# A down projection whose VectorE and ScalarE work is pinned to the program's order, with six weight-row buffers

## The chip, the cores and the metric

The kernel runs on one core of a Trainium2 chip. The metric is the device time of one execution in microseconds (us). Before the change it is 1452.64 us, the median of three runs (1451.81 to 1452.75).

## What is computed

One decoder layer for 256 tokens of width 2048, all in float32. A norm and an input projection feed a state-space branch and an attention branch; an output projection joins them to `x`; a convolutional feed-forward follows, and a last norm. The change touches only the end:

```
h = rms_norm(x, ffn_norm_w)
u = causal_depthwise_conv(h @ w_up, ffn_conv_w, ffn_conv_b)   # 2048 -> 2 x 5632
gate, val = split(u)
x = x + (silu(gate) * val) @ w_down                           # 5632 -> 2048
return rms_norm(x, final_norm_w)
```

## The kernel before, in words

**Precision.** A float32 product is made of three TensorE products. ScalarE rounds a 128 x 1024 block of weights into a high part (`whi`, line 1193), VectorE subtracts that from the block for the low part (`wlo`, line 1199), and TensorE adds (activation high) x (weight high), (activation low) x (weight high) and (activation high) x (weight low). The pair "high part, then low part" of one block is its *preparation*.

**Steps.** The whole program is one list of steps. A step loads a weight block, prepares it, and multiplies by it. The main loop at the end of the program walks the list. At step i it issues the loads up to step i + 7, the preparation of step i + 3 (`AHEAD`), then the step's own `pre` hook, its matmuls, its `post` hook, and then some pieces of side work taken from a queue of generators (`tick`, two pieces for most steps):

```
for i in range(n):
    loads_to(i + LOADS)
    while pi < n and pi <= i + AHEAD and i > 2:
        for f_ in steps[pi].prep: f_()
        pi += 1
    ... s.pre(); s.mm(); s.post(); tick(...)
```

There are four row buffers for the loaded blocks (`RAWS`) and four pairs of high and low buffers (`SPLITS`). So the preparation of step i + 3 writes the buffers that the matmuls of step i - 1 read.

**Who sets the order.** The program's order is only a wish. A scheduler in the language orders each engine's instructions ahead of the run by its own estimate of when each is ready. Each engine then works through its fixed list. An instruction made through a `Pinned` handle (lines 70 to 91) can be tied behind the instruction traced before it on its engine: TensorE's handle `T` always does this, `V` (VectorE), `A` (ScalarE) and `S` (SyncE's DMA queue) do it while the list `pin` isn't empty. Before the change `pin` holds something for the first seven steps only. The loads of the down projection's rows (lines 1178 and 1244), the final norm's weight (line 1152) and the output's stores (line 1396) are issued through `nc.sync`, not through `S`.

**The down projection.** `w_down` has 44 blocks of 128 rows; each block is taken in two halves of 1024 columns, so there are two passes over the rows, here called the first and the second half. Two neighbouring blocks make a pair, and there are 22 pairs in each half. A pair marked p in `orders` is two plain steps of 12 matmuls of 512 columns each (`prod_steps`). A pair marked s (6 in the first half, 7 in the second) is worked by a scheme with seven products in place of eight (`seven_steps`), in four steps a, b, c, d of 6, 6, 6 and 3 matmuls. Their preparations are chained: `t1` (line 1248) subtracts within the first row ahead of a's high part, `t23` (lines 1253 and 1254) makes the block `q` ahead of c's, and `t4` (line 1259) makes `r` ahead of d's; b has no such step. In the second half the order of pairs is pp, s p, four times s pp, s p, s ppp.

**Side work there.** `gather` and `sums` (lines 1281 to 1288, then a split at lines 95 and 96) make sums of activations for the seven s pairs, in three pieces each, 21 in all. A p step of the first half takes one piece while its row number is under 36, else two; s steps take none. `merge` (lines 1337 and 1338) adds the s pairs' banks into `x1` in four pieces after the last s pair of each half. `down_evac` (line 1360) adds a bank into `x1` and `square` (line 1354) sums its squares; `post0` does both four times at the end of the first half. `weigh` (line 1368) multiplies two quarters of `x1` by the final norm's weight `fnw`, which line 1427 scales by -0.5 first. `last_mm` ends the second half in an order of its own, with `finish_tokens` (lines 1385 to 1396) writing the output.

**Places.** `hcatf0` to `hcatf3`, the up projection's input, lie in four 8 KB places (per partition) H0 to H3. In the down projection H1 holds the scratch `tq`, H2 and H3 hold sums, and H0 holds `fnw`. Each pair's activations `act0` to `act21` have a 4 KB place of their own.

Of the kernel before, what the change touches and what calls it, by code (L numbers as in the profile page):

```python
# [10 lines left out]
F32 = mybir.dt.float32  # L11
F32R = mybir.dt.float32r
# [4 lines left out]
P = 128  # L17
D = 2048
L = 256
# [6 lines left out]
NHID = 256  # L26
NSH = 32
EPS = 1e-6
AHEAD, LOADS, WARM, FILL = 3, 7, 7, 2
RAWS, SPLITS, LATE = 4, 4, 4  # L30
R_SSM = 1.75
RATE = {"b": 2, "c": 2, "dt": 2, "x": 2, "ck": 1, "cv": 1, "q": 1.55, "z": 1.55}
# [11 lines left out]
def hymba_kernel(  # L44
# [22 lines left out]
    def wide(slot, shape, dtype, name):  # L67
        return gp.tile(shape, dtype, tag=f"H{slot}", name=name)
# [103 lines left out]
    small = lambda tag: gp.tile([P, 4, 3], F32, tag=tag, name=tag)  # L172
    for tag in ("nm1", "sm0", "sm1"):
        small(tag)
    hc = [wide(i, [P, 4, 2, L], F32R, f"hcat{i}") for i in range(4)]
    gp.tile([P, 16], F32, tag="pad", name="gpad")
    hcat = lambda k: hc[k // 4][:, k % 4]

    mixc = const.tile([P, NK], F32, name="mixc")

# [853 lines left out]
    x1 = [None] * 4  # L1034
    xsq = const.tile([P, NT, 4], F32, name="xsqs")
    hc2 = [None] * 4
    hcat2 = lambda k: hc2[k // 4][:, k % 4]

    def transpose_x1(c):
        yield from pause(WAIT["x1"])  # L1040
        for kk in range(4):
            k = 4 * c + kk
            if kk == 0:
                hc2[c] = wide(c, [P, 4, 2, L], F32R, f"hcatf{c}")
            ps = aux_bank()
            for t in range(NT):
                T.transpose(ps[:, t * P:(t + 1) * P], x1[c][:, t, kk * P:(kk + 1) * P], ident)
            split_scaled(hcat2(k)[:, 0], hcat2(k)[:, 1], ps[:, 0:256], pcol(O_FN + k))
            yield
# [97 lines left out]
    fnw = []  # L1147
    tqs = []

    def load_fnw():  # L1150
        ft = wide(0, [P, 4, 512], F32, "fnw")
        nc.sync.dma_start(ft.rearrange("p c e -> p (c e)"), final_norm_w.partition_broadcast(P))
        fnw.append(ft)

    def prod_steps(src, np_, pr, act, banks, first, last):

        for kl in range(2):
            k = 2 * pr + kl

            def mm(hf, w, k=k, kl=kl, ids=((0, 0), (0, 1), (1, 0), (1, 1))):  # L1160
                hv, lv = w
                x_ = banks["x"]
                if not x_:
                    x_.extend(banks["xb"]() for _ in range(4))
                for t, n in ids:
                    for hl in range(2):
                        T.matmul(x_[2 * t + n], act(k)[:, hl, t * P:(t + 1) * P], hv[:, n],
                                 start=(first and kl == 0 and hl == 0), stop=False)
                for t, n in ids:
                    T.matmul(x_[2 * t + n], act(k)[:, 0, t * P:(t + 1) * P], lv[:, n],  # L1170
                             start=False, stop=(last and kl == 1))

            s = Step()

            def load(k=k, s=s):
                raw = stage.tile([P, 1024], F32, tag="raw", name="raw", bufs=RAWS)
                s.raw = raw.rearrange("p (n c) -> p n c", n=2)
                nc.sync.dma_start(raw, src[k * P:(k + 1) * P, np_ * 1024:(np_ + 1) * 1024])

            s.load = load  # L1180
            s.prep = halves(s, lambda s=s: s.raw)
            s.mm = lambda s=s, mm=mm: mm(0, s.w)
            s.mm_ids = lambda ids, s=s, mm=mm: mm(0, s.w, ids=ids)
            s.k = k
            s.post = s.pre = None
            s.ticks = 2 - (np_ == 0 and k < 36)
            steps.append(s)
# [16 lines left out]
    def seven_steps(src, np_, pr, parts, banks, first, last):  # L1204

        st = {}  # L1210

        def product(bank, a_, w, n, x_first=False):
            (hv, lv), (ah, al) = w, a_()
            kw = dict(start=False, stop=False)
            T.matmul(bank, ah, hv[:, n], start=x_first, stop=False)
            T.matmul(bank, al, hv[:, n], **kw)
            T.matmul(bank, ah, lv[:, n], start=False, stop=last and any(bank is b for b in banks["y"]))

        def y(i):
            if not banks["y"]:  # L1220
                banks["y"].extend(banks["yb"]() for _ in range(4))
            return banks["y"][i]

        def mm_a(s):
            product(y(0), lambda: parts["a11"], s.w, 0, first)
            product(y(1), lambda: parts["s1"], s.w, 1, first)

        def mm_b(s):
            product(banks["x"][0], lambda: parts["a12"], s.w, 0)
            product(banks["x"][1], lambda: parts["s4"], s.w, 1)  # L1230

        def mm_c(s):
            product(y(2), lambda: parts["s2"], s.w, 0, first)
            product(y(3), lambda: parts["s3"], s.w, 1, first)

        def mm_d(s):
            product(banks["x"][2], lambda: parts["a22"], s.w, 0)

        def load_row(kl):
            def load():  # L1240
                raw = stage.tile([P, 1024], F32, tag="raw", name="raw", bufs=RAWS)
                st[kl] = raw.rearrange("p (n c) -> p n c", n=2)
                k = 2 * pr + kl
                nc.sync.dma_start(raw, src[k * P:(k + 1) * P, np_ * 1024:(np_ + 1) * 1024])
            return load

        def t1():
            V.tensor_tensor(st[0][:, 1], st[0][:, 1], st[0][:, 0], op=ALU.subtract)  # L1248

        def t23():  # L1250
            q_ = tqs[0][:, 0]
            st["q"] = q_
            V.tensor_tensor(q_[:, 0], st[1][:, 1], st[0][:, 1], op=ALU.subtract)
            V.tensor_tensor(q_[:, 1], q_[:, 0], st[0][:, 0], op=ALU.subtract)

        def t4():
            q_ = tqs[0][:, 1]
            st["r"] = q_
            V.tensor_tensor(q_[:, 0], st[1][:, 0], st["q"][:, 0], op=ALU.subtract)  # L1259

        def ready():
            while "a22" not in parts:
                tick(1)

        for mm, load, pre, key, n in ((mm_a, load_row(0), t1, 0, 2), (mm_b, load_row(1), None, 1, 2),
                                      (mm_c, None, t23, "q", 2), (mm_d, None, t4, "r", 1)):
            s = Step()
            s.load = load
            hl = halves(s, lambda key=key: st[key], n)
            s.prep = ((pre,) if pre else ()) + hl  # L1270
            s.mm = lambda s=s, mm=mm: mm(s)
            s.post = None
            s.pre = ready if key == 0 else None
            s.ticks = 0
            steps.append(s)
# [88 lines left out]
    def weigh():  # L1364
        for c in range(2):
            for t in range(NT):
                yield
                V.tensor_tensor(x1[c][:, t], x1[c][:, t], fnw[0][:, c], op=ALU.mult)
        yield

    fpart = const.tile([P, NT], F32, name="fpart")
# [6 lines left out]
    def finish_tokens(t, ssq_, more):  # L1378

        v, p_, f = (const.tile([P, 1], F32, name=f"fin{n_}{t}") for n_ in "vpf")
        r_ = const.tile([P, 1], F32, name=f"finr{t}")
        A.activation(r_, ssq_, AF.Sqrt, bias=more, scale=1.0 / D)
        V.tensor_scalar(v, ssq_, 1.0 / D, more, op0=ALU.mult, op1=ALU.add)
        V.reciprocal(r_, r_)
        V.scalar_tensor_tensor(p_, r_, v, r_, op0=ALU.mult, op1=ALU.mult)
        V.scalar_tensor_tensor(f, p_, -3.0, r_, op0=ALU.add, op1=ALU.mult)
        for q, (c, c0, n) in enumerate(((2, 0, 256), (0, 0, 512), (2, 256, 256), (1, 0, 512), (3, 0, 512))):  # L1390
            o_ = x1[c][:, t, c0:c0 + n]
            if c < 2:
                A.activation(o_, o_, AF.Copy, scale=f)
            else:
                V.scalar_tensor_tensor(o_, o_, f, fnw[0][:, c, c0:c0 + n], op0=ALU.mult, op1=ALU.mult)  # L1395
            nc.sync.dma_start(out[t * P:(t + 1) * P, c * 512 + c0:c * 512 + c0 + n], o_)

    orders = ["ppp" + "spp" * 5 + "sppp", "pp" + "sp" + "spp" * 4 + "sp" + "sppp"]
# [23 lines left out]
            banks["n"] = len(steps)  # L1422

    steps[n_down].pre = start_down
    steps[down[0]["n"]].pre = lambda: aux.append(weigh())
    steps[n_down + 2].pre = load_fnw
    steps[n_down + 36].pre = lambda: [A.activation(fnw[0][:, c], fnw[0][:, c], AF.Copy, scale=-0.5) for c in range(4)]
    steps[n_down + 64].pre = lambda: load_sqrt(fsq[:, 0, 0:1])
    last = steps[-LATE:]
    for i, s_ in enumerate(last[:-1]):  # L1430
# [69 lines left out]
    steps[6].post, steps[3].post = steps[3].post, None  # L1500
    credit = 0.0
    for i in range(n):
        loads_to(i + LOADS)
        while pi < n and pi <= i + AHEAD and i > 2:
            if steps[pi].late and pi > i + AHEAD - 1:
                break
# [3 lines left out]
        s = steps[i]  # L1510
        if s.pre:
            s.pre()
        if i < 3:
            s.mm_pass(0)
            steps[pi].prep[0]()
            split_x(range(4 * i + 4, 4 * i + 8))
            steps[pi].prep[1]()
            pi += 1
            s.mm_pass(1)
            if i == 1:  # L1520
                square_x((1,))
        else:
            s.mm()
# [45 lines left out]
```

## Time and profile before

| | |
|---|---|
| median of the runs | 1452.64 us |
| the profiled execution | 1451.33 us, its span 1449.7 us |
| TensorE (PE) busy | 1437.4 us, 99% |
| weight load into TensorE (PEld) | 1346.8 us, 93% |
| VectorE (DVE) busy | 1101.1 us, 76% |
| ScalarE (ACT) busy | 844.7 us, 58% |
| GpSimd (POOL) busy | 3.6 us |
| mean granted TensorE clock | 0.998 |

The span runs from the first to the last instruction; the execution takes 1.6 us more. The down projection's matmuls begin at 1207.05 us of the span, its second half at 1323.6 us, and the last matmul starts at 1440.64 us. Matmuls overlap one another, so that a busy TensorE isn't TensorE at its fastest: what shows a stall is the distance between the starts of matmuls.

### The profile page before, as it was taken

To read this page: it belongs to the slowest core of one execution; us is meant where nothing else is said; L and a number is where in the kernel's file an instruction comes from. 1 tells how busy PE (TensorE), PEld (TensorE's weight loads), DVE (VectorE), ACT (ScalarE), POOL (GpSimd) and SP (SyncE) were. 2 spreads that over 40 slices of the span, in tenths; PEclk is the share of its full clock that TensorE was granted. 3 is DMA by queue.
4 is the path that set the end of the run, shared out by engine and by line. 5 is a ranking of instruction groups with operands and counts; after the bars stand their busy time and mean duration, and the time that the engine had idled before them with its cause. 6 is when DMAs were issued, how large, how long until landed. Compare 5 with 4: busy or idle time off the path is not lost.

```text
span 1449.7 us, 26506 instructions
## 1 busy us (share of the span) xinstructions
PE 1437.4 (99%) x10512; PEld 1346.8 (93%) x10512; DVE 1101.1 (76%) x1733; ACT 844.7 (58%) x1281; POOL 3.6 (0%) x19
## 2 busy tenths in 40 slices
PE   9999999999999999999999999999999999999997
PEld 9999998989999998888899999999999998788886
DVE  7899699757797898555477777777777779878877
ACT  6677456556687696444355555555555556555554
POOL 1000000000000000000000000000000000000000
PEclk9999999999999999999999999999999999999999
DMA  8657667775544547566566666666666665665654
GB/s 274 186 181 241 182 212 234 237 216 159 156 137 140 161 134 231 188 189 192 178 195 194 198 192 193 197 192 193 197 193 192 198 192 191 205 204 186 213 193 145
DMA packets 222699, 278.76 MB, mean 192 GB/s; under 512 B 13176, under 2 KB 186864, under 8 KB 222448
## 3 DMA queue, kind: packets, MB, share of 16 engines
q1 hardware_dynamic: 220800, 272.59, 61.4%
q10 hardware_dynamic: 1776, 4.50, 0.9%
q8 instruction: 82, 1.34, 0.4%
q14 instruction: 41, 0.34, 0.1%
HBM read 274.92 MB, written 2.13 MB: 191 GB/s over the span
## 4 chain that ended last, share of the span: by engine, by line
PE 93%; DVE 3%; ACT 2%; DMA 1%; issue 1%; DVEq 0%; ACTq 0%; SPq 0%
PE mm L89 79%; PE aux L89 13%; DMA raw<-in_w_down_dram 1%; DVE wlo L1199 1%; ACT p L813 1%; ACT whi L1193 0%; DVE wlo L348 0%; DVE p L789 0%; DVE x L1395 0%; ACT L813 0%; ACT junk L1354 0%; DVE x L1337 0%; DVE pt L96 0%; ACT whi L342 0%; DVE tq L1259 0%
## 5 line engine op out<-in xcount | busy, mean ns | idle before, releaser
L342 ACT ACTIVATE whi<-raw 128x1024 fp32r<-128x1024 f32 x408 | 430.8, 1058 | 415.7 <-PE mm L89 360.9
L348 DVE TENSOR_TENSOR wlo<-raw,whi 128x1024 fp32r<-128x1024 f32 x408 | 496.4, 1220 | 222.8 <-ACT whi L342 214.1
L89 PE MATMUL mm<-hcatf,whi 128*128 128x256 f32 x2816 | 348.5, 277 | 0.0
L89 PEld LDWEIGHTS mm<-hcatf,whi 128*128 128x128 f32 x2816 | 332.6, 188 | 0.1
L89 PE MATMUL mm<-hcat,whi 128*128 128x256 f32 (+1 forms) x2336 | 294.8, 279 | 0.0
L89 PEld LDWEIGHTS mm<-hcat,whi 128*128 128x128 f32 (+1 forms) x2336 | 280.9, 188 | 2.7 <-issue 0.7
L89 PE MATMUL mm<-hcatf,wlo 128*128 128x256 f32 x1408 | 188.5, 277 | 0.0
L89 PEld LDWEIGHTS mm<-hcatf,wlo 128*128 128x128 f32 x1408 | 172.8, 188 | 0.0
L89 PE MATMUL mm<-hcat,wlo 128*128 128x256 f32 (+1 forms) x1168 | 159.8, 278 | 0.0
L89 PEld LDWEIGHTS mm<-hcat,wlo 128*128 128x128 f32 (+1 forms) x1168 | 144.5, 187 | 0.2 <-DVE wlo L89 0.2
L1193 ACT ACTIVATE whi<-raw 128x1024 fp32r<-128x1024 f32 x88 | 91.8, 1057 | 66.9 <-DVE raw L1248 19.0
L1199 DVE TENSOR_TENSOR wlo<-raw,whi 128x1024 fp32r<-128x1024 f32 x88 | 105.7, 1221 | 13.0 <-ACT whi L1193 11.9
L89 PE MATMUL aux<-whi,act 128*128 128x512 f32 (+1 forms) x306 | 78.0, 388 | 1.2 <-ACT whi L1193 1.2
L89 PE MATMUL mm<-whi,act 128*128 128x512 f32 (+1 forms) x286 | 74.2, 387 | 0.0
L89 PEld LDWEIGHTS aux<-whi,act 128*128 128x128 f32 x306 | 57.1, 188 | 13.2 <-ACT whi L1193 1.5
L390 DVE TENSOR_TENSOR u<-mm,bc 128x256 f32<-128x256 f32 x88 | 37.3, 424 | 36.9 <-PE mm L89 35.6
L89 PE MATMUL mm<-whi,ya 128*128 128x512 f32 x256 | 64.3, 394 | 0.0
L89 PEld LDWEIGHTS mm<-whi,act 128*128 128x128 f32 x286 | 53.5, 188 | 11.0
L89 PE MATMUL mm<-whi,ys 128*128 128x512 f32 x256 | 63.2, 390 | 0.0
L89 PEld LDWEIGHTS mm<-whi,ys 128*128 128x128 f32 x256 | 48.1, 188 | 9.9
L89 PEld LDWEIGHTS mm<-whi,ya 128*128 128x128 f32 x256 | 47.5, 188 | 9.6
L89 PE MATMUL aux<-wlo,act 128*128 128x512 f32 (+1 forms) x153 | 43.8, 388 | 0.0
(324 smaller groups left out, 1516.1 us busy)
## 6 DMA issues: line engine op xcount, KB each, us to landing
raw<-in_w_up_dram SPq DMA_DIRECT2D x176, 512.0 KB, 4.5
raw<-in_w_in_dram SPq DMA_DIRECT2D x160, 512.0 KB, 3.8
raw<-in_w_down_dram SPq DMA_DIRECT2D x88, 512.0 KB, 4.9
raw<-in_w_out_dram SPq DMA_DIRECT2D x64, 512.0 KB, 4.7
acq<-acum_d ACTq DMA_DIRECT2D x8, 512.0 KB, 5.5
raw<-in_cmp_w_k_dram SPq DMA_DIRECT2D x8, 512.0 KB, 5.1
raw<-in_cmp_w_v_dram SPq DMA_DIRECT2D x8, 512.0 KB, 4.3
x<-in_x_dram SPq DMA_DIRECT2D x4, 512.0 KB, 6.9
```

The lines of the kernel that those rows point to most:

```text
L89: return lambda *a, **kw: tc.keep_in_program_order(fn(*a, **kw))
L342: A.activation(hv, s.raw, AF.Copy)
L348: V.tensor_tensor(lv, s.raw, s.w[0].bitcast(F32), op=ALU.subtract)
L390: V.tensor_tensor(u, ps, root, op=ALU.mult)
L813: A.activation(v_, v_, AF.Exp, bias=nm[t][:, h, b:b + 1], accum_out=sm[t][:, h, b:b + 1])
L1193: A.activation(hv[:, 0:n], src()[:, 0:n], AF.Copy)
L1199: V.tensor_tensor(lv[:, 0:n], src()[:, 0:n], s.w[0].bitcast(F32)[:, 0:n], op=ALU.subtract)
```

## The change

In the down projection, from its first step to the one before its last, `pin` holds an entry, so that everything issued through `V`, `A` and `S` there is tied to the program's order. The row loads keep `nc.sync`. The 8 KB place H0 becomes two places of 4 KB, H0a and H0b; `hcat0` and `hcatf0` become two tiles each, and every third row of the down projection is loaded into H0a or H0b in turn, the other rows into the four buffers as before. Loads are issued up to nine steps ahead there (`LOADS_DOWN`), starting nine steps ahead of the down projection. `fnw` becomes two tiles in the places of `act7` and `act8`, which are last read by the first four steps of the second half; it is loaded by two DMAs at the second half's step 4 in place of one at the first half's step 2, scaled at step 14 of the second half, and `weigh` joins the queue at step 18 of the second half in place of its step 0.

```diff
-AHEAD, LOADS, WARM, FILL = 3, 7, 7, 2
+AHEAD, LOADS, LOADS_DOWN, WARM, FILL = 3, 7, 9, 7, 2
...
+    def quad(c, name):
+        if c:
+            return wide(c, [P, 4, 2, L], F32R, f"{name}{c}")
+        return tuple(wide(f"0{h}", [P, 2, 2, L], F32R, f"{name}0{h}") for h in "ab")
...
-                hc2[c] = wide(c, [P, 4, 2, L], F32R, f"hcatf{c}")
+                hc2[c] = quad(c, "hcatf")
...
     def load_fnw():
-        ft = wide(0, [P, 4, 512], F32, "fnw")
-        nc.sync.dma_start(ft.rearrange("p c e -> p (c e)"), final_norm_w.partition_broadcast(P))
-        fnw.append(ft)
+        for i in range(2):
+            ft = big(act_slots[N_SEVEN[1] + i], [P, 2, 512], F32, f"fnw{i}")
+            nc.sync.dma_start(ft.rearrange("p c e -> p (c e)"),
+                              final_norm_w[i * 1024:(i + 1) * 1024].partition_broadcast(P))
+            fnw.append(ft)
+
+    rows_loaded = [0]
+
+    def row_buf():
+        m = rows_loaded[0]
+        rows_loaded[0] += 1
+        if m % 3 == 2:
+            return wide("0" + "ab"[m // 3 % 2], [P, 1024], F32, "raw0")
+        return stage.tile([P, 1024], F32, tag="raw", name="raw", bufs=RAWS)
...
-                raw = stage.tile([P, 1024], F32, tag="raw", name="raw", bufs=RAWS)
+                raw = row_buf()
...
-    steps[down[0]["n"]].pre = lambda: aux.append(weigh())
-    steps[n_down + 2].pre = load_fnw
-    steps[n_down + 36].pre = lambda: [A.activation(fnw[0][:, c], fnw[0][:, c], AF.Copy, scale=-0.5) for c in range(4)]
+    second = down[0]["n"]
+    steps[second + 4].pre = load_fnw
+    steps[second + 14].pre = lambda: [A.activation(weight(c), weight(c), AF.Copy, scale=-0.5) for c in range(4)]
+    steps[second + 18].pre = lambda: aux.append(weigh())
...
-        loads_to(i + LOADS)
+        loads_to(i + (LOADS_DOWN if i >= n_down - LOADS else LOADS))
...
         if s.pre:
             s.pre()
+        if i == n_down:
+            pin.append(1)
+        elif i == n - 1:
+            pin.clear()
```

More of the change, by code (lines that the diff above doesn't have):

```diff
@@ L174, in hymba_kernel, with of_quads @@
         small(tag)
-    hc = [wide(i, [P, 4, 2, L], F32R, f"hcat{i}") for i in range(4)]
+    def quad(c, name):
+        if c:
+            return wide(c, [P, 4, 2, L], F32R, f"{name}{c}")
+        return tuple(wide(f"0{h}", [P, 2, 2, L], F32R, f"{name}0{h}") for h in "ab")
+    def of_quads(quads):
+        return lambda k: quads[0][k // 2][:, k % 2] if k < 4 else quads[k // 4][:, k % 4]
+    hc = [quad(c, "hcat") for c in range(4)]
     gp.tile([P, 16], F32, tag="pad", name="gpad")
-    hcat = lambda k: hc[k // 4][:, k % 4]
+    hcat = of_quads(hc)
     mixc = const.tile([P, NK], F32, name="mixc")
@@ L1036, in hymba_kernel @@
     hc2 = [None] * 4
-    hcat2 = lambda k: hc2[k // 4][:, k % 4]
+    hcat2 = of_quads(hc2)
     def transpose_x1(c):
@@ L1148, in hymba_kernel @@
     tqs = []
+    weight = lambda c: fnw[c // 2][:, c % 2]
     def load_fnw():
-        ft = wide(0, [P, 4, 512], F32, "fnw")
-        nc.sync.dma_start(ft.rearrange("p c e -> p (c e)"), final_norm_w.partition_broadcast(P))
-        fnw.append(ft)
+        for i in range(2):
[10 more added lines that the diff above has]
+        return stage.tile([P, 1024], F32, tag="raw", name="raw", bufs=RAWS)
     def prod_steps(src, np_, pr, act, banks, first, last):
@@ L1240, in load @@
             def load():
-                raw = stage.tile([P, 1024], F32, tag="raw", name="raw", bufs=RAWS)
+                raw = row_buf()
                 st[kl] = raw.rearrange("p (n c) -> p n c", n=2)
@@ L1367, in weigh @@
                 yield
-                V.tensor_tensor(x1[c][:, t], x1[c][:, t], fnw[0][:, c], op=ALU.mult)
+                V.tensor_tensor(x1[c][:, t], x1[c][:, t], weight(c), op=ALU.mult)
         yield
@@ L1394, in finish_tokens @@
             else:
-                V.scalar_tensor_tensor(o_, o_, f, fnw[0][:, c, c0:c0 + n], op0=ALU.mult, op1=ALU.mult)
+                V.scalar_tensor_tensor(o_, o_, f, weight(c)[:, c0:c0 + n], op0=ALU.mult, op1=ALU.mult)
             nc.sync.dma_start(out[t * P:(t + 1) * P, c * 512 + c0:c * 512 + c0 + n], o_)
```

## The prediction, made before the change was run

> **What bounds the kernel now.** I read the page first, then busy times in the two halves of the down projection (columns: stretch, length, PE, PEld, DVE, ACT, POOL, PEclk, DMA share, GB/s), then VectorE's waits there, then those of TensorE's weight loads.
>
> ```profile
> PE 1437.4 (99%) x10512; PEld 1346.8 (93%) x10512; DVE 1101.1 (76%) x1733; ACT 844.7 (58%) x1281; POOL 3.6 (0%) x19
> ```
> ```profile
> 1207.05:1323.60 116.55, 115.36 (x506) 94.55 (x505) 97.22 (x142) 63.85 (x81) 0.00 (x0) 1.00 0.59 197
> 1323.60:1441.00 117.40, 117.27 (x526) 96.84 (x524) 94.19 (x114) 62.63 (x76) 0.00 (x0) 1.00 0.54 179
> ```
> ```profile
> DVE tq L1253 <- DMA raw<-in_w_down_dram: 20.4, 11, 2.5
> DVE wlo L1199 <- ACT whi L1193: 13.1, 17, 1.8
> DVE raw L1248 <- DMA raw<-in_w_down_dram: 5.5, 5, 2.3
> ```
> ```profile
> PEld aux L89 <- ACT whi L1193: 1.5, 1, 1.5
> PEld mm L89 <- DVE wlo L1199: 0.8, 2, 0.5
> PEld aux L89 <- DVE wlo L1199: 0.3, 1, 0.3
> ```
>
> TensorE bounds it: all its waits for weights there come to 1.5 + 0.8 + 0.3 = 2.6 us. VectorE waits 20.4 + 5.5 = 25.9 us for rows, and TensorE hardly feels it, since VectorE is busy for only 97.2 of 116.6 and 94.2 of 117.4 us and works up to three steps ahead. So the wider row buffering can win 2.6 us at most.
>
> TensorE's pace, from its own timeline (start, length, what):
>
> ```profile
> 1397.93 1.98 PE L89 MATMUL mm<-whi,act 128*128 128x512 f32 x8
> 1399.74 1.07 PE L89 MATMUL mm<-wlo,act 128*128 128x512 f32 x4
> 1400.65 1.52 PE L89 MATMUL mm<-whi,act 128*128 128x512 f32 x6
> ```
>
> From 1397.93 to 1400.65, a plain step's 12 matmuls take 2.72 us, 0.227 each. An s pair has 21: 4.76 us, of which a, b and c 1.36 each, d 0.68. A cycle s pp is 4.76 + 4 x 2.72 = 15.64 us, s p 10.2.
>
> **What the program's order does to VectorE.** An s pair in the scheduler's order, VectorE's list and then ScalarE's:
>
> ```profile
> 1268.26 0.69 DVE L1253 TENSOR_TENSOR tq<-raw 128x512 f32<-128x512 f32 x1 [2.33 <-DMA raw<-in_w_down_dram]
> 1268.87 1.22 DVE L1199 TENSOR_TENSOR wlo<-raw,whi 128x1024 fp32r<-128x1024 f32 x1
> 1270.01 0.68 DVE L1254 TENSOR_TENSOR tq<-tq,raw 128x512 f32<-128x512 f32 x1
> 1270.61 1.22 DVE L1199 TENSOR_TENSOR wlo<-raw,whi 128x1024 fp32r<-128x1024 f32 x1
> 1271.74 0.68 DVE L1259 TENSOR_TENSOR tq<-raw,tq 128x512 f32<-128x512 f32 x1
> 1272.35 1.82 DVE L1199 TENSOR_TENSOR wlo<-tq,whi 128x1024 fp32r<-128x1024 f32 x2
> 1274.90 1.23 DVE L1199 TENSOR_TENSOR wlo<-raw,whi 128x1024 fp32r<-128x1024 f32 x1 [0.74 <-ACT whi L1193]
> ```
> ```profile
> 1270.81 1.06 ACT L1193 ACTIVATE whi<-tq 128x1024 fp32r<-128x1024 f32 x1 [1.47 <-DVE tq L1254]
> 1272.54 0.63 ACT L1193 ACTIVATE whi<-tq 128x512 fp32r<-128x512 f32 x1 [0.68 <-DVE tq L1259]
> 1273.81 1.06 ACT L1193 ACTIVATE whi<-raw 128x1024 fp32r<-128x1024 f32 x1 [0.63 <-PE mm L89]
> ```
>
> While ScalarE makes c's high part (1270.81), VectorE does b's low part and `t4`; from 1268.26 to 1274 it never waits on the chain. In the program's order the list is `t1`, a's low part, b's, `t23`, c's, `t4`, d's. Directly behind `t1`, `t23` and `t4` stands an instruction that needs a high part which ScalarE can start only then. Behind that instruction VectorE queues the next low parts and the sums, and TensorE waits for those.
>
> From these rows: a low part in a row takes 1.14 (1268.87 to 1270.01), 512 columns 0.61 (1268.26 to 1268.87); VectorE's end to ScalarE 0.12 (1270.69 to 1270.81), ScalarE's end to VectorE 0.03 (1274.87 to 1274.90). `t23` is a dependent pair, 0.73 apart:
>
> ```profile
> 1412.47 0.69 DVE L1253 TENSOR_TENSOR tq<-raw 128x512 f32<-128x512 f32 x1 [1.19 <-DMA raw<-in_w_down_dram]
> 1413.20 0.69 DVE L1254 TENSOR_TENSOR tq<-tq,raw 128x512 f32<-128x512 f32 x1
> ```
>
> VectorE's time, waits included: a 0.69 + 0.12 + 1.06 + 0.03 + 1.14 = 3.04; b 1.14; c 0.73 + 0.69 + 0.12 + 1.06 + 0.03 + 1.14 = 3.77; d 0.69 + 0.12 + 0.63 + 0.03 + 0.61 = 2.08; and 0.45 because the next step's high part stands behind d's on ScalarE (1.06 + 0.03, less d's low part). That is 10.48. A cycle s pp takes VectorE 10.48 + 4 x 1.14 = 15.04 of TensorE's 15.64, s p 12.76 of 10.2.
>
> **First half: stalls of 9.4 us.** The sums come on top. Their second and first piece:
>
> ```profile
> 1226.28 0.28 DVE L1285 TENSOR_TENSOR tq<-arow 128x128 f32<-128x128 f32 x1
> ...
> 1227.32 0.69 DVE L1281 TENSOR_TENSOR arow<-act 128x512 f32<-128x512 f32 x1
> ```
>
> The second takes 1.04 (start to start), the first and the third, 512 columns each, 0.61 and some 0.65: 2.3 per s pair. The third's split on ScalarE runs beside the next plain low part and costs nothing; were that cover gone, 0.63 + 0.15 a pair. The 21 pieces fall six on the first six steps, four in each of the next three cycles, three in the fourth, none in the fifth. With four, a cycle is 15.04 + 4/3 x 2.3 = 18.1 against 15.64: 2.4 us of stall once the lead is used up, of which I take 2.2 for the first. With three it is 1.6, with none 0. The first s pair comes with the last up pair's work in front:
>
> ```profile
> 1209.20 0.75 DVE L390 TENSOR_TENSOR u<-mm,bc 128x256 f32<-128x256 f32 x2
> ...
> 1214.39 0.75 DVE L96 TENSOR_TENSOR act<-acc,act 128x256 fp32r<-128x256 f32 x2
> ```
>
> 1209.20 to 1215.06, less two low parts in between, is 3.6. Then three low parts (3.42), two pairs' sums (4.6), a, b, c (7.95), `t4` and d's high part (1.44): 21.0 us, where TensorE wants d at 6 x 2.72 + 3 x 1.36 = 20.4. With d's low part, 0.8. Sum: 0.8 + 2.2 + 2 x 2.4 + 1.6 = 9.4.
>
> **Second half: 8.0.** `post0` opens it; VectorE, then ScalarE:
>
> ```profile
> 1326.82 2.48 DVE L1360 TENSOR_TENSOR x<-aux,x 128x512 f32<-128x512 f32 x4
> ```
> ```profile
> 1327.54 0.64 ACT L1354 ACTIVATE junk<-x 128x512 f32<-128x512 f32 x1 [2.20 <-DVE x L1360]
> 1328.08 0.19 ACT L1354 ACTIVATION_READ_ACCUMULATOR junk<-x 128x1 f32 x1
> 1328.30 0.64 ACT L1354 ACTIVATE junk<-x 128x512 f32<-128x512 f32 x1
> ```
>
> Four squares 0.76 apart hold ScalarE until 3.9 us into the half; step 3's high part stands behind them, its low part ends at 6.1, and a, b, c, `t4` and d's high part (9.4) at 15.5, where TensorE is at 14.96: 0.8 with d's low part. The short cycle behind it owes 12.76 - 10.2: 2.4. The middle cycles fit, but `weigh` (4 x 0.61) puts one over by 1.0. The last short cycle starts with a full lead: 1.0.
>
> The end (adds of `merge`, then PE and DVE rows):
>
> ```profile
> L1337 DVE TENSOR_TENSOR x<-x,tq 128x512 f32<-128x512 f32 x6 | 4.1, 686 | 0.0
> ```
> ```profile
> 1433.59 0.39 PE L89 MATMUL mm<-wlo,act 128*128 128x512 f32 x1
> ...
> 1434.82 1.28 DVE L1360 TENSOR_TENSOR x<-mm,x 128x512 f32<-128x512 f32 x2
> ```
>
> Now the last low part precedes the last adds, which only keep L1360 waiting, 1434.82 - 1433.98 = 0.8. In the program's order all eight adds (some 0.69 each) precede it: six low parts and 8 adds are 12.3 us, where TensorE needs the last low part 2 x 2.72 + 2 x 1.36 + 0.68 + 0.45 = 9.3 after the last s pair. I take 2.8, for a small lead. Sum: 0.8 + 2.4 + 1.0 + 1.0 + 2.8 = 8.0.
>
> **The rest: 0.** The weight's DMA (128 x 2048 floats, 1 MB) becomes two of 512 KB and moves past some 60 row loads on SP; POOL has nothing there. It is issued ten steps before its use and lies beside row loads of the same size (size, time to landing):
>
> ```profile
> raw<-in_w_down_dram SPq DMA_DIRECT2D x88, 512.0 KB, 4.9
> ```
>
> Two times 4.9 us is under the 24 us it has. Were it late, ScalarE would block at its scaling, at most some 5 us. The scaling, 4 x 0.6, and the square root's table load lie on ScalarE, idle for nearly half the time. Six buffers let a row's load start a full cycle (six rows) earlier, 15 us before its use against 4.9 for landing: row waits go, and so do TensorE's 2.6. The split of H0 costs nothing.
>
> **Sum.** 1451.33 (span 1449.7 + 1.6) + 9.4 + 8.0 - 2.6 = 1466.1. The runs' median lies 1.3 above that execution, within what I can't tell anyway; I say 1466. Bounds of the stalls: 0 if every wait hides in the lead, and some 22 if each sums cycle pays its split too and no lead helps: 1448.7 to 1471.
>
> **Rivals.** *The lead covers it:* no new stall, and the row waits go: 1451.33 - 2.6 = 1448.7, to 1452 if a wait or two remain. For it: VectorE's 83% and 80% busy, and 25.9 us of row waits that free it. Against it: the waits of a pair, 1.21 + 1.21 + 0.78 + 0.45 = 3.65, come to 22 us in the first half, and 97.2 + 22 exceeds 116.6. It decides if they stay under 2 us a pair. The Trainium skill (Perfetto Trace Analysis, Optimization Strategy) reads a gap that repeats on the engine that should be saturated as too few buffers; by that the change would win. Here the repeating gap lies on VectorE, not on TensorE, so the trace bears it out for 2.6 us at most. *Only the short cycles and the end stall:* the sums fit in the first half after all: 1451.33 + 8.0 - 2.6 = 1456.7. Against it, the sum of 18.1 for 15.64. *Row loads too:* SP waits for one late buffer and holds the rows behind it. If each of 13 pairs waited 1 us more for its rows with VectorE now the bound: 1479. Against it, 15 us of margin. *It doesn't do what it says:* the row loads keep the unpinned handle, so the DMA issues are not put in order; they follow a ring of buffers anyway, price 0.
>
> **Chances.** Forecast 0.57 (own range 1459 to 1471), short cycles alone 0.17, row loads too 0.06, lead covers it 0.20. What a measurement tells from no change is about 0.2%, 2.9 us: the lead's case gives faster 0.06 and same 0.14; the others are slower, 0.80. The range 1453 to 1472 leaves out the lead's case and little more.
>
> **What would show it.** VectorE's waits for ScalarE's high part (13.1 us now) grow to over 40 and its waits for rows go to near 0; TensorE's starts are over 1 us late at steps d and the steps behind, in the first half above all; the last low part ends 2 to 3 us after TensorE is ready for it. If matmuls still start 0.227 apart through the s pairs, I am wrong.

## The result, and the profile after

The change makes the kernel slower: 1466.16 us, the median of four runs (1465.35 to 1467.06), against 1452.70 us. The ratio is 1.0094, with a 95% interval of 1.0077 to 1.0112. The profiled execution took 1465.35 us, 14.0 more than the one of before.

The page of the kernel after:

```profile
span 1463.6 us, 26487 instructions
PE 1443.1 (99%) x10512; PEld 1344.2 (92%) x10512; DVE 1103.6 (75%) x1733; ACT 840.7 (57%) x1281; POOL 3.6 (0%) x19
```

The two halves of its down projection (columns as in the prediction):

```profile
1207.15:1332.05 124.90, 119.91 (x511) 94.38 (x510) 102.31 (x151) 59.70 (x77) 0.00 (x0) 1.00 0.55 181
1332.05:1455.00 122.95, 118.54 (x520) 94.87 (x518) 93.57 (x112) 62.42 (x79) 0.00 (x0) 1.00 0.51 172
```

VectorE runs the same 1733 instructions as before. How much longer each half takes can't be read off these windows and those of before, because the window of before ends its first half too early: the second half of the kernel before begins at 1324.98 us, not at 1323.60. Its first matmul there, and the first one of the first half after the change, which its window misses:

```profile
1324.98 1.98 PE L89 MATMUL mm<-whi,act 128*128 128x512 f32 x8
```
```profile
1206.92 1.99 PE L89 MATMUL aux<-whi,act 128*128 128x512 f32 x8
```

By the starts of matmuls the first half takes 125.13 us (1206.92 to 1332.05) in place of 117.93 (1207.05 to 1324.98), 7.2 more, and the second half takes 122.80 us to its last matmul (1454.85) in place of 115.66 (1440.64), 7.1 more. What waits for what, VectorE first and then TensorE's weight loads:

```profile
DVE wlo L89 <- ACT whi L89: 46.8, 53, 2.2
```
```profile
PEld mm L89 <- DVE wlo L89: 8.4, 9, 3.2
PEld aux L89 <- ACT whi L89: 6.3, 6, 1.5
PEld aux L89 <- DVE wlo L89: 3.8, 8, 1.0
PEld mm L89 <- ACT whi L89: 2.2, 5, 0.6
```

(Pinned instructions carry the helper's line 89, so they are told apart by their tiles.) VectorE's waits for rows, 25.9 us before, are gone from the list. Its waits for high parts have grown from 13.1 to 46.8 us, and TensorE's for weights from 2.6 to 20.7. One s pair of the first half, VectorE's list, then ScalarE's, then TensorE's:

```profile
1253.88 1.23 DVE L89 TENSOR_TENSOR wlo<-raw,whi 128x1024 fp32r<-128x1024 f32 x1 [1.26 <-ACT whi L89]
...
1257.36 0.69 DVE L89 TENSOR_TENSOR tq<-raw 128x512 f32<-128x512 f32 x1
1258.08 0.69 DVE L89 TENSOR_TENSOR tq<-tq,raw 128x512 f32<-128x512 f32 x1
1259.98 1.23 DVE L89 TENSOR_TENSOR wlo<-tq,whi 128x1024 fp32r<-128x1024 f32 x1 [1.21 <-ACT whi L89]
1261.12 0.28 DVE L89 TENSOR_TENSOR tq<-arow 128x128 f32<-128x128 f32 x1
...
1262.06 0.68 DVE L89 TENSOR_TENSOR tq<-raw,tq 128x512 f32<-128x512 f32 x1
1263.52 0.69 DVE L89 TENSOR_TENSOR wlo<-tq,whi 128x512 fp32r<-128x512 f32 x1 [0.78 <-ACT whi L89]
1264.47 4.63 DVE L89 TENSOR_TENSOR wlo<-raw,whi 128x1024 fp32r<-128x1024 f32 x4 [0.26 <-ACT whi L89]
```
```profile
1258.89 1.06 ACT L89 ACTIVATE whi<-tq 128x1024 fp32r<-128x1024 f32 x1 [3.57 <-PE mm L89]
1262.86 0.63 ACT L89 ACTIVATE whi<-tq 128x512 fp32r<-128x512 f32 x1 [2.91 <-DVE tq L89]
```
```profile
1260.24 0.62 PE L89 MATMUL mm<-whi,sums 128*128 128x512 f32 x2
1261.26 0.50 PE L89 MATMUL mm<-wlo,sums 128*128 128x512 f32 x1 [0.40 <-DVE wlo L89]
1261.60 0.62 PE L89 MATMUL mm<-whi,sums 128*128 128x512 f32 x2
1262.06 0.39 PE L89 MATMUL mm<-wlo,sums 128*128 128x512 f32 x1
1263.54 0.73 PE L89 MATMUL aux<-whi,act 128*128 128x512 f32 x2 [1.09 <-ACT whi L89]
```

The row at 1253.88 is a's low part, 1.26 us after VectorE was free. `t23` is the pair at 1257.36; only behind it can ScalarE start c's high part (1258.89), and VectorE stands idle for 1.21 us. The same comes at d: `t4` at 1262.06, high part at 1262.86, 0.78 us idle. TensorE meets c's low part 0.57 us late (1261.26 where two matmuls after 1260.24 would be 1260.69) and d's high part 1.25 us late.

### The profile page after: what moved, and what is told of

Its sections match the earlier page's. It is cut to its first block, busy times and chain, and to the rows that moved or that the text cites. A ratio compares the mean times of both kernels' runs of the same rounds, so it can differ in the third digit from the quotient of the medians.

```text
span 1463.6 us, 26487 instructions
## 1 busy us (share of the span) xinstructions
PE 1443.1 (99%) x10512; PEld 1344.2 (92%) x10512; DVE 1103.6 (75%) x1733; ACT 840.7 (57%) x1281; POOL 3.6 (0%) x19
## 4 chain that ended last, share of the span: by engine, by line
PE 91%; DVE 5%; ACT 2%; issue 2%; ACTq 0%; DVEq 0%
PE mm L89 78%; PE aux L89 13%; DVE wlo L89 1%; ACT whi L89 1%; DVE tq L89 1%; ACT p L821 1%; DVE x L89 0%; DVE wlo L356 0%; DVE p L797 0%; DVE x L1416 0%; ACT L821 0%; DVE pt L96 0%; DVE raw L89 0%; ACT whi L350 0%; DVE u L398 0%
## 5 line engine op out<-in xcount | busy, mean ns | idle before, releaser
L350 ACT ACTIVATE whi<-raw 128x1024 fp32r<-128x1024 f32 x408 | 430.7, 1058 | 415.2 <-PE mm L89 363.7
L89 PE MATMUL mm<-hcatf,whi 128*128 128x256 f32 x2112 | 261.3, 276 | 0.0
L89 PEld LDWEIGHTS mm<-hcatf,whi 128*128 128x128 f32 x2112 | 249.4, 188 | 0.0
L89 PE MATMUL mm<-hcat,whi 128*128 128x256 f32 (+1 forms) x1752 | 220.8, 278 | 0.0
L89 PEld LDWEIGHTS mm<-hcat,whi 128*128 128x128 f32 (+1 forms) x1752 | 210.2, 188 | 1.7 <-issue 0.5
L89 PE MATMUL mm<-hcatf,wlo 128*128 128x256 f32 x1056 | 141.2, 276 | 0.0
L89 PEld LDWEIGHTS mm<-hcatf,wlo 128*128 128x128 f32 x1056 | 129.6, 188 | 0.0
L89 PE MATMUL mm<-hcat,wlo 128*128 128x256 f32 (+1 forms) x876 | 119.7, 277 | 0.0
L89 ACT ACTIVATE whi<-raw 128x1024 fp32r<-128x1024 f32 (+1 forms) x95 | 94.3, 1041 | 41.8 <-DVE raw L89 28.0
L89 PEld LDWEIGHTS mm<-hcat,wlo 128*128 128x128 f32 (+1 forms) x876 | 108.2, 187 | 0.2 <-DVE wlo L89 0.2
```

The costliest lines, as they stand in the source:

```text
L89: return lambda *a, **kw: tc.keep_in_program_order(fn(*a, **kw))
L350: A.activation(hv, s.raw, AF.Copy)
```

## The experiments

Theory *bare chain*: held to the program's order, VectorE waits for each high part of the s pairs, has no slack left for that, and TensorE waits for VectorE. Rivals: *buffers* (the ring of six, the order of loads or the weight's new place cost the time) and *ScalarE's order*.

**The buffers and moves without the pinning.**

```diff
-        if i == n_down:
-            pin.append(1)
-        elif i == n - 1:
-            pin.clear()
```

> All of the change but the pinning: six row buffers, the split place H0, the moved weight and its later product, in the scheduler's order. Theory 'bare chain' (VectorE, held to the program's order, waits for each high part of the s pairs): the stalls go, 1450 to 1453 us, VectorE's waits for high parts fall from 46.8 us to some 13. Rival 'buffers' (the ring of six, the load order or the moved weight cost the time): 1464 to 1467. Since TensorE's waits before were 2 us in all, neither expects less than 1450.

Measured 1454.5 us, ratio to before 1.0016 [1.0007, 1.0026]. The 12 us go with the pinning, so *buffers* falls. But it is 1.5 us above the range and slower than before: six buffers did not rid the scheduler's order of row waits. They moved. VectorE's waits and a stretch of its list:

```profile
DVE raw L1269 <- DMA raw<-in_w_down_dram: 24.7, 9, 4.5
DVE wlo L1220 <- ACT whi L1214: 11.5, 14, 1.6
DVE tq L1274 <- DMA raw<-in_w_down_dram: 5.9, 9, 1.2
```
```profile
1257.06 0.69 DVE L1269 TENSOR_TENSOR raw<-raw 128x512 f32<-128x512 f32 x1 [0.78 <-DMA raw<-in_w_down_dram]
1257.67 0.28 DVE L96 TENSOR_TENSOR sums_bc<-tq,sums_bc 128x128 fp32r<-128x128 f32 x1
1258.94 0.69 DVE L1274 TENSOR_TENSOR tq<-raw 128x512 f32<-128x512 f32 x1 [0.98 <-DMA raw<-in_w_down_dram]
1259.55 0.69 DVE L1220 TENSOR_TENSOR wlo<-tq,whi 128x512 fp32r<-128x512 f32 x1
1260.15 0.69 DVE L1275 TENSOR_TENSOR tq<-tq,raw 128x512 f32<-128x512 f32 x1
1260.75 0.68 DVE L1280 TENSOR_TENSOR tq<-raw,tq 128x512 f32<-128x512 f32 x1
1261.35 0.29 DVE L96 TENSOR_TENSOR act<-tq,act 128x128 fp32r<-128x128 f32 x1
1261.55 4.62 DVE L1220 TENSOR_TENSOR wlo<-raw,whi 128x1024 fp32r<-128x1024 f32 x4
```

The scheduler puts `t1` to `t4` of a coming pair ahead of four plain steps' low parts (1261.55). There they wait for rows that have not landed, and the low parts behind them come late, the one of the pair before (1259.55) first. The moved weight waits here as well: ScalarE waits 3.7 us for its two DMAs and VectorE 1.9 us for its scaling, about 1337 us into the span, but no matmul starts late between 1297 and 1353 us.

**The pinning without the buffers.** The same five lines added to the kernel before.

> The kernel before with the pinning alone: four row buffers, the weight in H0. 'Bare chain': at least the 1466 of the whole change, and up to 5 us more where four buffers add row waits to a VectorE that has no slack. 'Buffers': as before, 1452 to 1454.

Measured 1476.71 us, the median of two runs, ratio 1.0167 [1.0147, 1.0187]: the whole change's 1466 and 10.5 us more, above the 5 that were expected. So in this order the six buffers do work, and the row load is a second chain: ScalarE waits 16.0 us for rows in all, VectorE behind it for the high part. ScalarE's and VectorE's rows of one step b:

```profile
1255.68 1.06 ACT L89 ACTIVATE whi<-raw 128x1024 fp32r<-128x1024 f32 x1 [1.58 <-DMA raw<-in_w_down_dram]
```
```profile
1256.77 1.23 DVE L89 TENSOR_TENSOR wlo<-raw,whi 128x1024 fp32r<-128x1024 f32 x1 [1.34 <-ACT whi L89]
```

Not all of the 10.5 us is rows. This kernel also keeps `weigh` at the second half's start, where its four products stand among the preparations of the first s pair. Two of its rows, three products:

```profile
1340.64 0.68 DVE L89 TENSOR_TENSOR x<-x,fnw 128x512 f32<-128x512 f32 x1
1344.25 1.29 DVE L89 TENSOR_TENSOR x<-x,fnw 128x512 f32<-128x512 f32 x2
```

TensorE loses 2.5 us at that pair, where the whole change loses 0.1 there and 1.0 at a later pair that has the products instead. By these stalls some 1.4 of the 10.5 us comes from the weight's place, an estimate, and some 9 from the rows.

**Pinned in the second half only.**

```diff
-        if i == n_down:
+        if i == second:
             pin.append(1)
```

> The whole change, but pinned from the second half on only. 'Bare chain': the first half's stalls (9.0 us by the distance of matmuls) go, the short cycles', weigh's and the end's (7.1) stay: 1457. 'Buffers': 1466. A theory in which only short cycles and the end stall also expects 1466.

Measured 1457.93 us, ratio 1.0038 [1.0022, 1.0054], three runs. By the medians, pinning the first half carries 8 of the 13.5 us; a theory of short cycles and the end alone falls. The first half's stalls don't go altogether: by the distance of matmuls they fall from 9.0 to 2.7 us, with VectorE waiting for rows in the scheduler's order again.

**The chain covered.** In `seven_steps` the subtraction goes between the high and the low part of the preparation before its own:

```diff
-            s.prep = ((pre,) if pre else ()) + hl
+            s.prep = hl
+            if pre:
+                steps[-1].prep = steps[-1].prep[:1] + (pre,) + steps[-1].prep[1:]
```

> The whole change, pinned, but with each subtraction t1, t23 and t4 written one low part earlier, between the high and the low part of the preparation before its own, so that ScalarE makes the next high part while VectorE does that low part. No instruction more or less. 'Bare chain': a pair's 3.65 us of waits go, VectorE's waits for high parts fall under 12 us, the stalls of the first half, the short cycles and weigh go, and only the end's adds ahead of the last low part stay, 1.5 to 3 us: 1451 to 1455. 'Buffers': 1466. A rival 'ScalarE's order' (its program order, not VectorE's, stalls) expects no more than a few us of gain, 1460 or more.

Measured 1450.21 us, ratio 0.9984 [0.9974, 0.9993]: 16 us from the order of three subtractions per pair, with everything still pinned. TensorE has one wait for weights left, at the last low part, 1.5 us. One point missed: VectorE's waits for high parts fell to 25.2 us, not under 12. What is left is VectorE ahead of ScalarE, which itself waits 64 us for TensorE to free its buffers; that costs TensorE nothing.

**One engine pinned at a time.**

```diff
-            if not (pin or self.always):
+            if not (pin or (down_pin and self.eng is nc.vector) or self.always):
```

and in the loop `down_pin` in place of `pin`; for the second kernel `nc.scalar`.

> The whole change with only VectorE pinned; ScalarE's order is left to the scheduler. 'Bare chain': VectorE still meets each high part bare, 1463 to 1467. 'ScalarE's order': 1451 to 1455.

> The whole change with only ScalarE pinned; VectorE's order is left to the scheduler. 'Bare chain': the scheduler puts other work under the high parts again, 1450 to 1455. 'ScalarE's order': 1463 to 1467.

Measured 1466.60 us with VectorE alone (two runs), ratio 1.0099 [1.0080, 1.0117], and 1455.12 us with ScalarE alone, 0.1 above its range, ratio 1.0016 [1.0005, 1.0028]. `S` is pinned in neither, so the order of the DMA queue is no part of it. VectorE's order does it all; ScalarE's does nothing that can be told from the kernel without any pinning (1.0016 too). *ScalarE's order* falls.

**The second half of the last merge taken late.**

```diff
+    for s_ in steps[-5:]:
+        s_.ticks = 0
...
     def last_mm():
-        drain()
...
         down_evac(3)(0, x_[1])
+        drain()
```

> The whole change, but the second four adds of the second half's merge are taken after the first two banks of the last stretch have been added (down_evac of quarters 2 and 3 for the first 128 tokens) instead of ahead of the last low part. 'Bare chain' with the end as forecast (eight adds ahead of the last low part stall TensorE 2.9 us): that stall goes or falls under 0.5, 1463. Rival: the adds only move, the end of the span waits for them behind the last matmul, 1465.5 to 1466.5.

Measured 1462.70 us, ratio 1.0073 [1.0058, 1.0089], 3.5 us under the whole change, 3.0 by the ratios. TensorE at the last step, with the whole change and then with this edit:

```profile
1444.26 0.61 PE L89 MATMUL mm<-whi,act 128*128 128x512 f32 x2
1447.65 0.50 PE L89 MATMUL mm<-wlo,act 128*128 128x512 f32 x1 [2.77 <-DVE wlo L89]
```
```profile
1444.25 0.61 PE L89 MATMUL mm<-whi,act 128*128 128x512 f32 x2
1444.86 0.50 PE L89 MATMUL mm<-wlo,act 128*128 128x512 f32 x1
```

The wait for the last low part falls from 2.94 us, counted by starts, to 0.16, and the end of the span doesn't pay it back.

**Both edits.**

> Both edits: the subtractions one low part earlier, and the second four adds late. If the chain and the end are all there is, no stall of TensorE over 0.5 us is left in the down projection: 1450 us, 0.1 to 0.2% under the kernel before. Rival: something else in the program's order (ScalarE's squares and scaling, the last up pair's work) still stalls: 1453 or more.

Measured 1448.78 us, ratio 0.9976 [0.9966, 0.9985]: faster than both kernels, 3.5 us or 0.24% under the one before, a little more than expected. TensorE's halves in it, within 0.4 us at their edges:

```profile
1207.05:1323.00 115.95, 115.95 (x512) 95.69 (x511) 101.98 (x151) 62.62 (x77) 0.00 (x0) 1.00 0.61 198
1323.00:1438.00 115.00, 115.00 (x518) 95.39 (x517) 93.17 (x111) 64.72 (x79) 0.00 (x0) 1.00 0.55 180
```

TensorE is busy for all of both, and its weight loads wait for nothing.

**Both edits on four buffers.** The kernel of the pinning alone with the two edits above.

> The kernel before (four row buffers, the weight in H0, the weighing at the second half's start), pinned, with the subtractions one low part earlier and the second four adds late: what the six buffers are worth once the chain is covered. If the row waits of four buffers in program order (10.5 us beside the whole change with pinning alone) come from VectorE having no slack, they hide again: 1449 to 1451. If they come from the order of the loads and the time that a row needs to land, they stay in part: 1453 to 1459.

Measured 1449.30 us, ratio 0.9977 [0.9968, 0.9987], not to be told from 0.9976 with six. VectorE still waits for rows:

```profile
DVE wlo L89 <- ACT whi L89: 15.3, 14, 1.8
DVE raw L89 <- DMA raw<-in_w_down_dram: 13.3, 9, 2.5
```

TensorE waits for none of it. What four buffers cost beside six with the bare chain, some 9 us, came from a VectorE without slack, not from the loads as such.

## Why the prediction was right, point by point

The forecast was 1466 and the time 1466.16. That they agree to 0.2 us is luck. The sum starts from the profiled execution of before and so forecasts the profiled one after, which took 1465.35 us: the sum was 0.8 too high, and the median of the runs happens to lie 0.8 above that execution. Its parts can be read off the starts of matmuls: what a distance holds over 0.227 us per matmul (0.12 for 256 columns) is a stall.

- **First half, 9.4 forecast, 9.0 measured.** At the six s pairs in turn: 0.7, 2.0, 2.3, 2.4, 1.6 and 0, where 0.8, 2.2, 2.4, 2.4, 1.6 and 0 were forecast. The mechanism is shown: the same instructions with the chain covered have none of it, and pinning VectorE alone has all of it. The pair shown above waits 1.26 + 1.21 + 0.78 + 0.26 = 3.51 us for high parts, where 3.65 were forecast.
- **Second half, 8.0 forecast, 7.3 measured.** The first s pair 0.1 for 0.8, the short cycle behind it 2.4 for 2.4, `weigh`'s cycle 1.0 for 1.0, the last short cycle 0.8 for 1.0, the end 3.0 for 2.8. The first of them was mis-sized. It let the four adds of `post0` begin at the half's start and ScalarE's squares end 3.9 us into it. The adds began 0.5 us earlier, as the first bank is finished ahead of the others (1331.57, the half begins at 1332.05), and step 3's high part started at 1335.19, 3.1 us in.
- **The row waits, -2.6.** TensorE's lost distances before were 2.1 us, 0.5 less than its waits, and the last matmul's start moved by 9.0 + 7.3 - 2.1 = 14.2 us, as its rows say (1440.64 and 1454.85). Where the step went wrong is its reason: "the wider row buffering can win 2.6 us". In the scheduler's order the six buffers, with the moved weight, won nothing and cost 2 us; and once the chain was covered, four gave the same time as six. Here they were needed only where VectorE had no slack.
- **The rest, 0.** The weight's DMAs, its scaling and the table load appear in no wait of VectorE or TensorE in the whole change.
- **The rivals.** *The lead covers it* fell with 46.8 us of waits in VectorE's list: 3.5 us at the pair shown, where it needed under 2. *Row loads too* fell for six buffers; with four it is what happened, for some 9 us, so the margin of a full cycle that six buffers give was the right thing to weigh. *Only the short cycles and the end* fell with pinning in the second half. That the DMA issues are not put in order was true and cost nothing that a run here shows.

The signs named beforehand came: waits for high parts over 40 us, none for rows in VectorE's list, d's high part 1.25 us late at the pair shown, and the last low part 2.9 us late.

What stays open: why the scheduler, given six buffers, places `t1` to `t4` so much earlier than their rows land. The runs show that it does and what follows, not its estimate.

## What to carry to other kernels

An engine at 80% busy can have no room for program order if that order puts a producer on another engine directly between two of its own instructions: count such hand-overs with their round trip (here 0.12 + 1.06 + 0.03 us) as busy time, and compare the sum per cycle with the pace of the bound. The remedy is in the order written down, not in leaving it to a scheduler: one independent instruction of about the same length between the two hid nearly all of the hand-over, and a pinned order that is right beat the scheduler's by 3.5 us here. Count buffers only after that; here a lack of them showed mostly where the engine had no slack.

## What the hardware showed that was not expected

A stall of TensorE holds a little more than its wait. Behind the first matmul after a wait the next one starts 0.34 us later (1261.26 and 1261.60 in the rows above) in place of 0.227, some 0.11 us per wait. At d there are two waits, one behind the other, as d's low part is ready only after its high part. The weight load of its third matmul shows the second:

```profile
1264.26 0.19 PEld L89 LDWEIGHTS aux<-wlo,act 128*128 128x128 f32 x1 [0.43 <-DVE wlo L89]
```

The first half has 14 such restarts, some 1.5 us. I had not counted them apart; they lie in the stalls above. Why a restart costs this is not shown.

In some profiled executions a slower clock came with a wait. With ScalarE alone pinned, TensorE's rows around a wait of 1.98 us, and windows just after it and later (PEclk is the third figure from the right):

```profile
1262.76 0.50 PE L89 MATMUL aux<-wlo,act 128*128 128x512 f32 x1 [1.98 <-DVE wlo L1220]
1263.10 2.91 PE L89 MATMUL aux<-whi,act 128*128 128x512 f32 x8
1265.80 1.80 PE L89 MATMUL aux<-wlo,act 128*128 128x512 f32 x4
1267.44 1.78 PE L89 MATMUL aux<-whi,act 128*128 128x512 f32 x7
```
```profile
1262.50:1267.50 5.00, 4.74 (x14) 3.74 (x15) 5.00 (x7) 2.92 (x6) 0.00 (x0) 0.66 0.27 85
1267.50:1272.50 5.00, 5.00 (x24) 4.10 (x23) 4.93 (x12) 1.35 (x2) 0.00 (x0) 1.00 0.86 294
```

The granted clock was 0.66 in the mean over these 5 us; in the 3.4 us from 1263.93 to 1267.33 it was 0.50, and 1.00 on both sides. The 12 matmuls from 1263.10 to 1267.44 took 4.34 us in place of 2.72. The profiled execution with VectorE alone pinned has such a stretch from 1264.00, at the end of a wait of 1.49 us, and the one pinned in the second half only has one from 1439.80, at the end of the wait for the last low part:

```profile
1439.94 0.79 PE L89 MATMUL mm<-wlo,act 128*128 128x512 f32 x1 [2.79 <-DVE wlo L89]
```

Each of these three profiled executions holds some 1.5 us of it. The whole change's own wait of 2.77 us at the same place left the clock at 1.00. So the length of the wait doesn't decide it here; what does is not shown. The Trainium skill (TensorE: Matmul & The Clock Gate, HAM oscillation — how this bites in real kernels) gives gaps over about 3.4 us as those that bring the clock down. The traces here differ: waits of 1.49, 1.98 and 2.79 us came with the slower clock.
